# Layer 0's conditioning in its paired products: two places, half steps, an earlier start

## The chip, the cores and the metric

The kernel runs on one core of one Trainium2 chip. The metric is the device time of one execution in microseconds (us). The engines are TensorE (PE; its weight loads are shown as PEld), VectorE (DVE), ScalarE (ACT), GpSimd (POOL) and SyncE (SP). Transfers are issued from a queue of SP, ACT or POOL, and each engine and each queue works in its own fixed order.

## The reference

One inference step of a two-layer trunk over 640 tokens (512 latent tokens and 128 prompt tokens) of width 2048. In each layer, in outline:

```
sh, sc, gt = split(silu(cond) @ ada_w[layer] + ada_b[layer], 3)   # cond: one row for the prompt, one for the latents
h = rms_norm(x, norm_g[layer]) * (1 + sc) + sh
y = mixer(h @ w_in)          # layer 0: windowed attention, and a gated width-3 convolution
x = x + gt * (y @ w_out)     # layer 1: differential attention, and grouped attention
```

The part that matters here is the first line, the *conditioning*: two rows of 2048 numbers times a matrix of 2048 x 6144 per layer, which has to be read whole from HBM (50 MB a layer). Its result for layer 1 is needed only when layer 1's `h` is made.

## The kernel before, in words

**Projections.** The large products multiply 128 x 128 weight tiles by 320 token columns at a time (two halves of the 640 tokens). For accuracy each factor is split into a high and a low part: ACT rounds the weights to `wh` (L292), DVE subtracts to get `wl` (L293), and PE forms three products per tile. Layer 0's input projection first runs as *single tiles* (`run_tiles`): one column block of 128 at a time, four *quarters* of 24 matmuls each. The last nine twice-wide column blocks run as *pairs* (`run_pairs`): two column blocks at once, with seven products M1, M5, M6, M2, M7, M3, M4 in the place of eight, in that order. Each product has 24 matmuls over 320 columns (L612 to L614) in two halves. Some products need sums of weights, which DVE makes: L551 for M5, L554 and L556 for M6 and M7, L563 for M3. A pair loads its weights into tiles of the tag `w8` (four places) and of `raw`.

**The order of the work.** The kernel is written as Python generators. After each quarter of a single tile, and after each half of a pair's product, `slot()` is called. It advances `prep` (what follows a tile), then `attn` (attention, or here `forms`, which prepares moving operands for the pairs), and then a *filler* `fill`: `credit` grows by `rate`, and for each whole unit of credit one step of the filler is written out. The order on each engine follows from the order in which instructions are written and from when a scheduler thinks that they can run; it is fixed when the kernel is built. Low parts of weights are written three quarters, or three half products, ahead of their use (`SPLIT_AHEAD`), raw weights of single tiles five quarters ahead.

**The turn.** At single tile `n_turn` of layer 0 (L471) six single tiles are left: four gates, one `u` and one `c`. There `tail_turn` (L1338) empties the first filler, closes one pool of tiles and opens the next, `mid`, with five places of the tag `xr`, and queues `forms`. The filler's rate becomes 0 for these six tiles. The gates take three `xr` tiles each. In the last of the six, `twist` (L1347) overwrites half of `h` with `t1`, for which part of the constant tile `tables` is used.

**The conditioning beside the pairs.** `ada_slow` (L265) is the filler of the pairs, with a rate of 0.33. It computes two blocks of 512 columns for layer 1. For each of 16 weight tiles of 128 x 512 (256 KB) of a block, one step does two DVE operations, one for each of the two conditioning rows: L279 for the first weight tile, L281 for the others:

```
V.scalar_tensor_tensor(out=acc[c], in0=w, scalar=sT[:, kt, c:c + 1], in1=acc[c],
                       op0=ALU.mult, op1=ALU.add)
```

and then fetches the next weight tile through POOL's queue (L270) into the same place `w`, a part of `tables`. After a block `ada_fold` (L224) sums the accumulators over the partitions on PE (L229), copies the sums on ACT, turns them on PE (L235) and adds the bias on DVE. At M6 of the last pair `tail_tail` (L1392) writes out whatever is left of the filler, and queues the first four tiles of the output projection's operand (`late_yin`, L1181), which take `xr` places too.

Of the kernel before, what the change touches and what calls it, by code (L numbers as in the profile page):

```python
# [15 lines left out]
ALU = mybir.AluOpType  # L16
# [6 lines left out]
KT = D // P  # L23
# [3 lines left out]
HALF = NT // 2  # L27
# [23 lines left out]
FILL0_FROM = 6  # L51
# [5 lines left out]
def trunk_kernel(ctx: ExitStack, tc: tile.TileContext, I: dict, O: dict):  # L57
# [206 lines left out]

    def ada_slow(blocks):  # L265

        w = tables[:, 3 * HALF:3 * HALF + 512]

        def fetch(l, cb, kt):
            nc.gpsimd.dma_start(w, I["ada_w"][l, kt * P:(kt + 1) * P, cb * 512:(cb + 1) * 512])  # L270

        fetch(*blocks[0], 0)
        yield
        for b, (l, cb) in enumerate(blocks):
            acc = [xr_tile(f"acc{c}")[:, 0:512] for c in range(2)]
            for kt in range(KT):
                for c in range(2):
                    if kt == 0:
                        V.tensor_scalar(acc[c], w, sT[:, kt, c:c + 1], None, ALU.mult)  # L279
                    else:  # L280
                        V.scalar_tensor_tensor(out=acc[c], in0=w, scalar=sT[:, kt, c:c + 1], in1=acc[c],  # L281
                                               op0=ALU.mult, op1=ALU.add)
                if kt + 1 < KT:
                    fetch(l, cb, kt + 1)
                elif b + 1 < len(blocks):
                    fetch(*blocks[b + 1], 0)
                yield
            ada_fold(l, cb, acc, pools["cur"], "xr", 5)
            yield

    def split(hi, lo, x):
        A.activation(hi, x, AF.Copy)  # L292
        V.tensor_sub(lo, x, hi)  # L293
# [73 lines left out]
    def slot(fill=None, rate=0.0, steps=1.0):  # L367
        settle_late()
        advance(prep, len(prep))
        pace[0] += steps  # L370
        while pace[0] >= 1.0:
            advance(attn, 1)
            pace[0] -= 1.0
        credit[0] += rate
        while credit[0] >= 1.0:
            next(fill, None)
            credit[0] -= 1.0

    def run_tiles(jobs, w_ap, make_h, fill=None, rate=0.0, ahead=None, order=(0, 1, 2, 3), before=None,
# [89 lines left out]
        for i in range(lead, len(jobs)):  # L469
            fn = jobs[i][1]  # L470
            if turn and i == turn[0]:  # L471
                drain(prep)
                turn[1]()
                rate = 0.0
            pp = new_pp((i - lead) % 2)
            if twist and i == len(jobs) - 1:
                for hv in (HV[1:], HV[:1]):
                    for qd in range(4):
                        proj_q(pp, parts[t + qd], qd, qd, hv)
                        run_ahead(t + 1)  # L480
                        slot(fill, rate / 2, steps(i) / 2)
                    if hv[0][0]:
                        twist()
                drain(prep)
                begin(fn, pp)
                return (i - lead) % 2
            split_last = last is not None and i == len(jobs) - 1
            for qd in range(4):
                proj_q(pp, parts[t], qd, qd, HV[:1] if split_last else HV)
                if before and qd == 0:  # L490
                    before(i)
                t += 1
                run_ahead(t)
                if pending and not prep:
                    n = pending.pop(0)
                    begin(jobs[n][1], pps[n])
                slot(fill, rate if t > fill_from else 0.0, steps(i))
            if split_last:
                first = last(pp, 0)
                next(first)  # L500
                for qd in range(4):
                    proj_q(pp, parts[t - 4 + qd], qd, qd, HV[1:])
                    next(first, None)
                for _ in last(pp, 1):
                    pass
                return
            drain(prep)
            if i >= lead + grace and pending:
                settle()
            if lp and not pending and not prep:  # L510
                lp.__exit__(None, None, None)
                lp = None
            begin(fn, pp)
# [2 lines left out]

    GROUP = {"M1": "M1", "M6": "M1", "M7": "M1", "M4": "M1", "M5": "M5", "M3": "M5", "M2": "M2"}

    def run_pairs(cols, w_ap, mov, room, used, begin, done, tail, fill=None, rate=0.0):


        ap = pools["cur"]
# [79 lines left out]
        for i, (p, name) in enumerate(seq):  # L602
            if name in ("M1", "M5", "M2"):
                bank = {"M1": f"pa{(used + p + 1) % 2}", "M5": f"pb{1 - used}", "M2": f"pb{used}"}[name]
                banks[name] = pproj.tile([P, 512], F32, tag=bank, name="pq")[:, 0:HALF]
            ps, rows_ = banks[GROUP[name]], mov[MOV[name]]
            first, final = name in GROUP.values(), name in ("M4", "M3", "M2")
            for h in range(2):
                wh, wl = parts[2 * i + h]
                for j in range(4):  # L610
                    hi, lo = rows_(4 * h + j)
                    PE.matmul(ps, wh[:, j, :], hi, start=(first and h == 0 and j == 0), stop=False, skip_group_check=True)  # L612
                    PE.matmul(ps, wh[:, j, :], lo, start=False, stop=False, skip_group_check=True)  # L613
                    PE.matmul(ps, wl[:, j, :], hi, start=False, stop=(final and h == 1 and j == 3),  # L614
                              skip_group_check=True)
                if h == 0:
                    ahead(2 * i + 1)
                    slot(fill, rate)
            after(p, name, ps)
            ahead(2 * i + 2)  # L620
            if name == "M1":
                load(p + 1, "A11")
            elif name == "M6":
                load(p + 1, "A21")
                load(p + 1, "A22")
            elif name == "M7":
                load(p + 1, "A12")
            if p == len(cols) - 1:
                tail(name)
            slot(fill, rate)  # L630

    def stage(ap, pp):
        s = ap.tile([P, NT], F32, tag="stg", name="stg", bufs=2)
# [499 lines left out]
    def forms(src):  # L1133

        f = None

        def load(j):
            if src is None:
                for k, n in ((j, "acc"), (j + 8, "sq")):
                    V.tensor_add(st[n], *hs[k])  # L1140
                return st["acc"], st["sq"]
            ts = [big("w8", bufs=4)[:, 0:NT] for _ in range(2)]
            for i in range(2):
                nc.sync.dma_start(ts[i], src[j + 8 * i])
            return ts

        T.clear()
        t1.clear()
        nxt = load(0) if src else None
        for j in range(8):  # L1150
            (ya, yb), nxt = nxt or load(j), (load(j + 1) if src and j < 7 else None)
            b11, b12, b21, b22 = ya[:, 0:HALF], ya[:, HALF:NT], yb[:, 0:HALF], yb[:, HALF:NT]
            x = big("sx")[:, 0:3 * HALF]
            if f is None:
                f = big("sf")
            d = room[j] if j < 4 else f[:, (j - 4) * HALF:(j - 3) * HALF] if j < 7 else b11
            x2, x3, x4 = (x[:, i * HALF:(i + 1) * HALF] for i in range(3))
            V.tensor_sub(x3, b22, b12)
            V.tensor_add(x2, b11, x3)
            V.tensor_sub(x4, b21, x2)  # L1160
            V.tensor_sub(d, b12, b11)
            t = big(f"T{j}", dtype=F32R).rearrange("p (s n) -> p s n", s=2)
            split(t[:, 0, :], t[:, 1, :], x)
            T.append(t)
            t1.append(d)
            yield
# [119 lines left out]
    def xr_tile(name):  # L1286
        return pools["cur"].tile([P, NT], F32, tag="xr", name=name, bufs=5)
# [50 lines left out]
    def tail_turn():  # L1338
        drain(attn)
        for _ in fill0:  # L1340
            pass
        close("even")
        open_pool("mid")
        st["acc"], st["sq"] = (pools["cur"].tile([P, NT], F32, tag=n, name=n) for n in ("acc", "sq"))
        attn.append(forms(None))

    def twist():  # L1347
        drain(attn)
        for j in range(8):
            hi, lo = hs[j]  # L1350
            split(hi[:, HALF:NT], lo[:, HALF:NT], t1[j])

    used = run_tiles(jobs, I["ev_w_in"][0], h0_maker, fill0, FILL0, ada_group, trans=TRANS, grace=GRACE,
                     cut=((0, 2), (2, 4)), summed=keep, led=even_start, lead_in=lambda: ada_on_pe(0, 0, 0, 2),
                     steps=lambda i: 0.4 if i >= n_turn else 1.35 if i > last_q else 1.0,
                     turn=(n_turn, tail_turn), twist=twist, fill_from=FILL0_FROM)

    tails = [("b", "h", 3)] + [x for i in range(4, 8) for x in (("u", "c", i), ("b", "h", i))]
    srcs = {}
# [32 lines left out]
    def tail_tail(name):  # L1392
# [7 lines left out]
        elif name == "M3":  # L1400
            for n in range(2):
# [2 lines left out]
    run_pairs([(EV[a] + i * P, EV[b] + i * P) for a, b, i in tails], I["ev_w_in"][0],  # L1404
              {"B11": half_of(0, 0), "T1": half_of(0, 1), "B21": half_of(8, 0), "B22": half_of(8, 1),
               "T2": form_of(0), "T3": form_of(1), "T4": form_of(2)}, room, used, tail_begin, tail_done, tail_tail,
              fill0b, 0.33)
    drain(prep)

    def y0_maker(k):  # L1410
# [410 lines left out]
```

## Time and profile before

| what | us |
|---|---|
| median of 3 runs | 2278.35 (2276.54 to 2283.84) |
| profiled execution | 2275.12 |
| its span, first to last instruction | 2273.3 |
| PE busy in it | 2230.9 (98%) |
| DVE busy in it | 1712.6 (75%) |
| layer 0's last six single tiles, about | 567 to 653 |
| layer 0's pairs | 653.4 to 887.1 |

Times inside the profile are counted from the span's start. In a row of a view, "L281 DVE" is the source line and the engine, `out<-in` are the kernel's names of tiles, and what stands in square brackets is the time that the engine stood idle just before, and what ended it. Instructions are pipelined, so that the next one can start a little before the end that is shown for the one before. The mean granted clock of PE in this execution was 0.996.

### The profile page before, as it was taken

The page shows a single profiled execution, that of the slowest core. Times are in us where ns is not written, and L with a number is a line of the kernel's source. Part 1 is how long each engine was busy: PE and PEld are TensorE (multiplying, and loading weights), DVE is VectorE, ACT ScalarE, POOL GpSimd, SP SyncE. Part 2 cuts the span into 40 slices and gives each one's busy share as a digit, 9 for nine tenths or more (in the row PEclk, how much of TensorE's full clock was granted, in tenths as well). Part 3 has the DMA queues.
Part 4 walks back from the last instruction along what each step waited for, and adds up shares of the span by engine and source line. Part 5 has one row for each costly group of instructions (what it writes and reads, how often), then busy time and mean ns, then how long its engine had stood idle before and what let it go on. Part 6 is the DMA issues. An engine that isn't in the chain of part 4 may idle for free.

```text
span 2273.3 us, 41407 instructions
## 1 busy us (share of the span) xinstructions
PE 2230.9 (98%) x15708; PEld 2156.4 (95%) x15708; DVE 1712.6 (75%) x3197; ACT 1109.6 (49%) x2293; POOL 225.3 (10%) x337
## 2 busy tenths in 40 slices
PE   7999999999999999999999999999999999999999
PEld 5889999999999999999999999999999999999999
DVE  4659899988868898887776764858658778676665
ACT  4335554544333435444644445566665554554443
POOL 2220000000001000000200000010010111111010
PEclk9999999999999999999999999999999999999999
DMA  9985556564534447743763334423324234237541
GB/s 357 340 284 156 175 171 204 164 188 151 157 100 130 135 122 227 210 140 113 246 211 115 108 110 141 132 71 99 94 76 145 76 115 131 78 114 245 168 134 49
DMA packets 385607, 351.43 MB, mean 155 GB/s; under 512 B 18162, under 2 KB 342224, under 8 KB 384896
## 3 DMA queue, kind: packets, MB, share of 16 engines
q1 hardware_dynamic: 369008, 289.76, 42.5%
q0 software_dynamic: 15536, 56.80, 7.2%
q8 instruction: 123, 2.02, 0.4%
q10 hardware_dynamic: 864, 2.23, 0.3%
q14 instruction: 76, 0.62, 0.1%
HBM read 305.86 MB, written 42.86 MB: 153 GB/s over the span
## 4 chain that ended last, share of the span: by engine, by line
PE 50%; DVE 6%; ACT 3%; issue 2%; DMA 2%; POOL 1%; ACTq 0%; DVEq 0%; POOLq 0%; SPq 0%
PE pq L612 8%; PE pq L613 8%; PE pq L614 8%; PE pb L328 3%; PE pb L327 3%; PE pa L329 3%; PE pb L329 3%; PE pa L328 3%; PE pa L327 3%; DVE acc L218 1%; PE T L642 1%; PE T L815 1%; DMA adaw<-in_ada_w 1%; DVE nm L789 1%; ACT p L796 1%
## 5 line engine op out<-in xcount | busy, mean ns | idle before, releaser
L292 ACT ACTIVATE wh<-raw 128x512 fp32r<-128x512 f32 (+1 forms) x400 | 241.1, 604 | 393.5 <-PE pb L328 277.3
L327 PE MATMUL pa<-h,wh 128*128 128x320 f32 x1216 | 388.7, 320 | 0.4 <-DVE sum L416 0.4
L328 PE MATMUL pa<-h,wh 128*128 128x320 f32 x1216 | 379.0, 312 | 1.5 <-DVE h L293 1.5
L327 PE MATMUL pb<-h,wh 128*128 128x320 f32 x1216 | 378.1, 311 | 0.9 <-ACT h L292 0.9
L329 PE MATMUL pa<-h,wl 128*128 128x320 f32 x1216 | 377.9, 311 | 0.0
L329 PE MATMUL pb<-h,wl 128*128 128x320 f32 x1216 | 377.8, 311 | 0.0
L328 PE MATMUL pb<-h,wh 128*128 128x320 f32 x1216 | 377.4, 310 | 0.0
L293 DVE TENSOR_TENSOR wl<-raw,wh 128x512 fp32r<-128x512 f32 (+1 forms) x400 | 261.2, 654 | 142.2 <-ACT wh L292 126.5
L612 PE MATMUL pq<-h,wh 128*128 128x320 f32 x896 | 277.4, 310 | 0.0
L614 PE MATMUL pq<-h,wl 128*128 128x320 f32 x896 | 277.1, 309 | 0.0
L613 PE MATMUL pq<-h,wh 128*128 128x320 f32 x896 | 276.6, 309 | 0.0
L327 PEld LDWEIGHTS pa<-h,wh 128*128 128x128 f32 x1216 | 228.9, 188 | 10.6 <-issue 9.7
L328 PEld LDWEIGHTS pa<-h,wh 128*128 128x128 f32 x1216 | 229.3, 189 | 6.5 <-issue 4.5
L327 PEld LDWEIGHTS pb<-h,wh 128*128 128x128 f32 x1216 | 229.5, 189 | 2.1 <-ACT h L292 1.1
L329 PEld LDWEIGHTS pa<-h,wl 128*128 128x128 f32 x1216 | 228.8, 188 | 1.6 <-issue 1.6
L328 PEld LDWEIGHTS pb<-h,wh 128*128 128x128 f32 x1216 | 229.4, 189 | 0.4 <-issue 0.4
L329 PEld LDWEIGHTS pb<-h,wl 128*128 128x128 f32 x1216 | 229.2, 188 | 0.4 <-issue 0.4
L612 PE MATMUL pq<-T,wh 128*128 128x320 f32 x672 | 209.3, 311 | 3.4 <-ACT wh L292 1.8
L614 PE MATMUL pq<-T,wl 128*128 128x320 f32 x672 | 208.3, 310 | 2.7 <-DVE wl L293 2.7
L613 PE MATMUL pq<-T,wh 128*128 128x320 f32 x672 | 208.2, 310 | 0.0
L258 DVE SCALAR_TENSOR_TENSOR acc<-adaw,sT,acc 128x1024 f32<-128x1024 f32 x150 | 189.1, 1275 | 0.0
L292 ACT ACTIVATE wh<-sx 128x512 fp32r<-128x512 f32 x168 | 105.1, 632 | 151.7 <-PE pq L613 96.2
(375 smaller groups left out, 4682.7 us busy)
## 6 DMA issues: line engine op xcount, KB each, us to landing
adaw<-in_ada_w SPq DMA_DIRECT2D x80, 512.0 KB, 4.0
raw<-in_od_w_in SPq DMA_DIRECT2D x160, 256.0 KB, 3.0
raw<-in_ev_w_in SPq DMA_DIRECT2D x130, 256.0 KB, 3.5
ada<-in_ada_w SPq DMA_DIRECT2D x11, 2048.0 KB, 13.5
adaw<-in_ada_w SPq DMA_DIRECT2D x128, 128.0 KB, 2.4
w<-in_ev_w_in SPq DMA_DIRECT2D x27, 512.0 KB, 3.9
w<-in_od_w_in SPq DMA_DIRECT2D x24, 512.0 KB, 4.0
adah<-in_ada_w SPq DMA_DIRECT2D x20, 512.0 KB, 9.2
```

The source lines that it names most:

```text
L218: V.scalar_tensor_tensor(out=a, in0=w, scalar=sT[:, kt, c:c + 1], in1=a, op0=ALU.mult, op1=ALU.add)
L258: V.scalar_tensor_tensor(out=acc[c], in0=w, scalar=sT[:, kt, c:c + 1], in1=acc[c], op0=ALU.mult, op1=ALU.add)
L292: A.activation(hi, x, AF.Copy)
L293: V.tensor_sub(lo, x, hi)
L327: PE.matmul(ps, wh[:, i, :], hi[:, sl], start=(j == js[0] if alone else (pos == 0 and j == 0)), stop=False)
L328: PE.matmul(ps, wh[:, i, :], lo[:, sl], start=False, stop=False)
L329: PE.matmul(ps, wl[:, i, :], hi[:, sl], start=False, stop=(j == js[1] - 1 if alone else (pos == 3 and j == 3)))
L612: PE.matmul(ps, wh[:, j, :], hi, start=(first and h == 0 and j == 0), stop=False, skip_group_check=True)
L613: PE.matmul(ps, wh[:, j, :], lo, start=False, stop=False, skip_group_check=True)
L614: PE.matmul(ps, wl[:, j, :], hi, start=False, stop=(final and h == 1 and j == 3), skip_group_check=True)
L642: PE.transpose(t[:, i * P:(i + 1) * P], src(b), ident)
L789: V.tensor_reduce(nm, s, axis=AX.X, op=ALU.max, negate=True)
```

## The change

`ada_slow` gets two places instead of one and fetches two weight tiles ahead. Its places depend on the time: until `twist` it takes a new `w8` tile for each fetch (`st["adaw"]`), and after that it alternates between the old place in `tables` and one `xr` tile. One step is now one DVE operation instead of two (a *half step*), and a new fetch is written after the second of a weight tile.

`run_tiles` no longer sets the rate to 0 at the turn: it takes a new filler and rate from `turn`, here `fill0b` (this `ada_slow`) and 0.7, so that the conditioning begins beside the last six single tiles. `run_pairs` no longer takes a rate: it advances the filler by one half step in each of the two slots of the products named in `rests`, here M6, M2 and M3, and not in the others.

```
     def ada_slow(blocks):
-        w = tables[:, 3 * HALF:3 * HALF + 512]
-        def fetch(l, cb, kt):
+        todo = [(l, cb, kt) for l, cb in blocks for kt in range(KT)]
+        places, ws = [], []
+        def fetch():
+            if not todo:
+                return
+            l, cb, kt = todo.pop(0)
+            if "adaw" in st:
+                w = st["adaw"]()
+            else:
+                if not places:
+                    places.extend([tables[:, 3 * HALF:3 * HALF + 512], xr_tile("adaw")[:, 0:512]])
+                w = places[0]
+                places.reverse()
             nc.gpsimd.dma_start(w, I["ada_w"][l, kt * P:(kt + 1) * P, cb * 512:(cb + 1) * 512])
-        fetch(*blocks[0], 0)
+            ws.append(w)
+        fetch()
+        fetch()
         yield
-        for b, (l, cb) in enumerate(blocks):
+        for l, cb in blocks:
             acc = [xr_tile(f"acc{c}")[:, 0:512] for c in range(2)]
             for kt in range(KT):
                 for c in range(2):
                     if kt == 0:
-                        V.tensor_scalar(acc[c], w, sT[:, kt, c:c + 1], None, ALU.mult)
+                        V.tensor_scalar(acc[c], ws[0], sT[:, kt, c:c + 1], None, ALU.mult)
                     else:
-                        V.scalar_tensor_tensor(out=acc[c], in0=w, scalar=sT[:, kt, c:c + 1], in1=acc[c],
+                        V.scalar_tensor_tensor(out=acc[c], in0=ws[0], scalar=sT[:, kt, c:c + 1], in1=acc[c],
                                                op0=ALU.mult, op1=ALU.add)
-                if kt + 1 < KT:
-                    fetch(l, cb, kt + 1)
-                elif b + 1 < len(blocks):
-                    fetch(*blocks[b + 1], 0)
-                yield
+                    if c:
+                        ws.pop(0)
+                        fetch()
+                    yield
             ada_fold(l, cb, acc, pools["cur"], "xr", 5)
             yield
...
 (run_tiles)
             if turn and i == turn[0]:
                 drain(prep)
-                turn[1]()
-                rate = 0.0
+                fill, rate = turn[1:3]
+                turn[3]()
...
 (run_pairs)
-    def run_pairs(cols, w_ap, mov, room, used, begin, done, tail, fill=None, rate=0.0):
+    def run_pairs(cols, w_ap, mov, room, used, begin, done, tail, fill=None, rests=()):
...
-                    slot(fill, rate)
+                    slot(fill, float(name in rests))
...
 (tail_turn)
+        st["adaw"] = lambda: big("w8", bufs=4)[:, 0:512]
         attn.append(forms(None))
...
 (twist)
+        st.pop("adaw")
...
-                     turn=(n_turn, tail_turn), twist=twist, fill_from=FILL0_FROM)
+                     turn=(n_turn, fill0b, 0.7, tail_turn), twist=twist, fill_from=FILL0_FROM)
...
-              fill0b, 0.33)
+              fill0b, ("M6", "M2", "M3"))
```

More of the change, by code (lines that the diff above doesn't have):

```diff
@@ L629, in run_pairs @@
                 tail(name)
-            slot(fill, rate)
+            slot(fill, float(name in rests))
     def stage(ap, pp):
```

## The prediction

> **What bounds the kernel now.** I read the page first, then busy time by stretch, then the waits of the engine that fell behind, then its timeline at a loss.
>
> ```profile
> span 2273.3 us, 41407 instructions
> PE 2230.9 (98%) x15708; PEld 2156.4 (95%) x15708; DVE 1712.6 (75%) x3197; ACT 1109.6 (49%) x2293; POOL 225.3 (10%) x337
> ```
>
> TensorE (PE) is the bound, so the change is worth only the PE time that it gives back. I cut the touched part at the starts of its nine pairs. The first row is the single tiles from shortly after their turn; the others are pairs 0 to 8 of layer 0. The columns are the width, then busy us and instruction count per engine, then the granted clock.
>
> ```profile
> core 0: us, PE busy (x) PEld busy (x) DVE busy (x) ACT busy (x) POOL busy (x), PEclk, DMA share, GB/s
> 571.00:653.40 82.40, 82.40 (x564) 82.40 (x563) 61.95 (x104) 29.03 (x49) 3.24 (x6) 1.00 0.47 139
> 653.40:678.00 24.60, 24.60 (x170) 24.60 (x169) 22.21 (x37) 10.87 (x19) 2.16 (x4) 1.00 0.41 115
> 678.00:706.20 28.20, 26.73 (x170) 26.20 (x169) 23.17 (x37) 9.89 (x18) 3.23 (x6) 0.94 0.50 146
> 706.20:730.80 24.60, 24.60 (x170) 24.60 (x169) 22.52 (x37) 10.78 (x19) 1.84 (x4) 1.00 0.40 118
> 730.80:759.10 28.30, 26.16 (x180) 25.00 (x179) 22.35 (x36) 10.26 (x19) 2.46 (x5) 1.00 0.43 125
> 759.10:783.80 24.70, 24.70 (x171) 24.70 (x170) 22.65 (x38) 10.89 (x19) 2.15 (x4) 1.00 0.38 111
> 783.80:809.20 25.40, 24.81 (x169) 24.58 (x169) 21.66 (x34) 10.01 (x18) 3.23 (x6) 1.00 0.49 147
> 809.20:836.90 27.70, 25.76 (x171) 24.70 (x170) 24.46 (x40) 10.57 (x19) 2.15 (x4) 1.00 0.39 115
> 836.90:862.50 25.60, 25.60 (x180) 25.00 (x179) 21.31 (x35) 10.28 (x19) 1.62 (x3) 1.00 0.51 156
> 862.50:887.10 24.60, 24.60 (x170) 24.60 (x170) 22.94 (x39) 17.15 (x29) 0.00 (x0) 1.00 0.57 174
> ```
>
> An undisturbed pair takes 24.60 us (pairs 0, 2 and 8). The others exceed it by 3.6, 3.7, 0.1, 0.8, 3.1 and 1.0, together 12.3 us. Two of them (3 and 7, with some ten instructions more) contain a fold of the conditioning, which is work and stays:
>
> ```profile
> 754.73 0.64 PE L229 MATMUL T<-acc,ones 128*32 128x256 f32 x8
> 756.58 0.38 PE L235 MATMUL T<-ident,ada_sb 128*128 128x128 f32 x2
> ```
>
> A fold is 0.64 + 0.38 = 1.02 us, two are 2.0, so **10.3 us of PE time are lost in the pairs**. The cause is on VectorE (DVE): the one place for a conditioning weight.
>
> ```profile
> DVE acc L281 <- DMA tables<-in_ada_w: 18.7, 19, 2.2
> L281 DVE SCALAR_TENSOR_TENSOR acc<-tables,sT,acc 128x512 f32<-128x512 f32 x60 | 43.8, 747 | 18.8 <-DMA tables<-in_ada_w 18.7
> L279 DVE TENSOR_SCALAR acc<-tables,sT 128x512 f32<-128x512 f32 x4 | 1.9, 480 | 0.0
> ```
>
> DVE stood still 19 times, 18.7 us in all, at the head of its queue for a weight to land. All of this falls in pairs 0 to 7. Their DVE busy times average 22.54 us; with 18.7 / 8 = 2.3 us of waiting that is 24.9 us against 24.6 us of PE work. DVE has nothing left, and what it queues behind the wait comes late:
>
> ```profile
> 680.52 1.42 DVE L281 SCALAR_TENSOR_TENSOR acc<-tables,sT,acc 128x512 f32<-128x512 f32 x2 [1.71 <-DMA tables<-in_ada_w]
> 681.85 0.48 DVE L1380 SCALAR_TENSOR_TENSOR acc<-sq,pq 128x320 f32<-128x320 f32 x1
> 682.25 0.68 DVE L293 TENSOR_TENSOR wl<-sx,wh 128x512 fp32r<-128x512 f32 x1
> 682.85 0.82 DVE L1382 TENSOR_TENSOR CV<-CV,acc 128x640 f32<-128x640 f32 x1
> 683.59 1.22 DVE L554 TENSOR_TENSOR sx<-sx,w 128x1024 f32<-128x1024 f32 x1
> 685.20 1.41 DVE L281 SCALAR_TENSOR_TENSOR acc<-tables,sT,acc 128x512 f32<-128x512 f32 x2 [0.40 <-DMA tables<-in_ada_w]
> 686.53 1.29 DVE L293 TENSOR_TENSOR wl<-sx,wh 128x512 fp32r<-128x512 f32 x2
> ...
> 685.58 0.41 PE L612 MATMUL pq<-T,wh 128*128 128x320 f32 x1 [0.34 <-ACT wh L292]
> 687.27 0.42 PE L614 MATMUL pq<-T,wl 128*128 128x320 f32 x1 [1.13 <-DVE wl L293]
> ```
>
> Ahead of M6's weight sum (L554) and its low part stand two waits (1.71 + 0.40) and four conditioning operations (1.42 + 1.41). PE then waits for exactly that high and low part: pair 1's loss.
>
> **The change part by part.** *Two places.* A fetch takes this long:
>
> ```profile
> L270 POOL DMA_DIRECT2D tables<-in_ada_w x32: 536/536/545, 642.7 to 843.9; - x32
> DMA to landing us min/median/max: 2.8/3.1/4.1
> ```
>
> Today it is issued after a step's second operation, for the next step three half-product slots on; a slot is 24.6 / 14 = 1.76 us, so 5.3 us are left and DVE's running order eats the margin. With two places a fetch goes out two weights ahead. In the pairs, the shortest way from fetch to use is from the end of M6 to the middle of M3, over M2 and M7: five slots, 8.8 us against at most 4.1. The 18.7 us of DVE waiting go.
>
> *Fewer and spread steps.* The generator now yields 67 times: one start, 64 half steps, two folds. By the code the turn leaves 0.2 of credit (82 slots at 2.1), and 20 slots at 0.7 and 8 at 0.35 add 16.8: 17 calls beside the single tiles, hence 16 half steps. The pairs call it in M6, M2 and M3 only, six times a pair: 48 half steps less one in pairs 0 to 7, then the last half step, a fold, and the drain after pair 8's M6. In pairs 0 to 7 the DVE load other than conditioning is 22.54 - (43.8 + 1.9) / 8 = 16.8 us; six operations at 0.747 make it 21.3 us of 24.6, with no wait inside. M4's end, M1 and M5, where all three large losses began, hold none. In M3, M2 and M7 a backlog of a few tenths is possible; the low parts are made three half products ahead (5.3 us), which covers it. If that cover were gone, each 0.1 us would cost 0.1 on PE. Of the 10.3 us I let 1.5 stay lost (pair 5, which has the smallest DVE load and still lost 0.8 us, is the nearest row).
>
> *The moved half steps.* Beside the single tiles PE is full (82.40 of 82.40), so whatever DVE delays there is a new loss.
>
> ```profile
> 571.00:617.00 46.00, 46.00 (x316) 46.00 (x315) 43.60 (x74) 17.00 (x26) 2.16 (x4) 1.00 0.60 178
> 617.00:653.40 36.40, 36.40 (x250) 36.40 (x249) 18.35 (x32) 12.03 (x23) 1.08 (x2) 1.00 0.30 89
> ```
>
> The half steps cost 2 x 0.48 + 14 x 0.747 = 11.4 us; DVE has 82.4 - 61.95 = 20.4 us free, but only 2.4 until 617, where forms() fills it. At 0.7 in a slot of 3.5 us, 46 us take some 9 half steps, 6.7 us: forms() ends about 4 us later than now (at 617), still ahead of the twist near 641. Low parts have three quarters, 10.5 us, of lead. I put this at 0, with 0 to 4 us as bounds. The 10 fetches (0.54 us each) go through POOL's queue past the gates' stores, an engine with 3.24 us busy in 82; 0.
>
> *w8 places.* The early fetches use the four places of the pairs' own weights, which four loads take long ahead today:
>
> ```profile
> 574.87 1.05 SPq L527 DMA_DIRECT2D w<-in_ev_w_in  x2
> 578.22 2.54 SPq L527 DMA_DIRECT2D w<-in_ev_w_in  x2
> ...
> w<-in_ev_w_in SPq DMA_DIRECT2D x23, 512.0 KB, 3.9
> ...
> L292 ACT ACTIVATE wh<-raw 128x512 fp32r<-128x512 f32 (+1 forms) x400 | 241.1, 604 | 393.5 <-PE pb L328 277.3
> ```
>
> Two are now held by conditioning until about 652, so A12 of pair 0 loads then and lands at about 656 to 658; its halves are split from about 660 for M2 at 664. Covered by some 3 us; 0, and if the 17th call slips behind the first M6 slot (662) it costs up to 662 + 3.9 + 1.3 - 664 = 3.2 us (load, then high part 0.60 and low part 0.65). SP's queue behind that load holds raw weights five quarters ahead.
>
> *The end.* The second fold moves from 851 to after pair 8's M6 (about 14 us before the pairs end), and its accumulators free the places of the first y tiles later. Now those are done early:
>
> ```profile
> 868.09 1.55 DVE L293 TENSOR_TENSOR h<-yin,h 128x640 fp32r<-128x640 f32 x2
> 873.24 0.81 DVE L293 TENSOR_TENSOR h<-yin,h 128x640 fp32r<-128x640 f32 x1
> ```
>
> 13 us before the projection needs them at 887. Fold, load and splits move them some 10 us; 3 us stay. Cost 0, up to 3. Each fold now follows its last half step by one slot, not three: PE may wait for DVE, between 0 and 1.76 us each; I take 0.4 each, as DVE has slack then.
>
> *Sum*: -10.3 + 1.5 + 0.8 = **-8.0 us**. The profiled execution took 2275.1 us (span 2273.3); the median shown is 2278.35, 3.2 above, and the saving is the same: 2278.35 - 8.0 = **2270.3 us**.
>
> One part of the 10.3 is clock. Pair 1's PE idled 28.20 - 26.73 = 1.5 us but lost 3.6: its granted clock was 0.94, so about 0.06 x 28.2 = 1.7 us went to slower matmuls; pair 3 idled longer (2.1 us) at 1.00. I take the drop as the wait's doing. The Trainium skill, TensorE: Matmul & The Clock Gate, "What's actually happening", says that the clock halves only after an idle window of about 3.4 us that runs freely; by that 1.5 us would not be enough, and the sum would be -6.3. This hangs on it: rival C.
>
> **The rivals.** *A, the steps are not moved* (25%). If pair loads take all w8 places first, nothing is fetched beside the single tiles, and DVE keeps 22.5 us per pair without waits: 92%. Or DVE still lags and M6 and M3 keep waiting. For: the four loads above go out at the turn. Against: the first fetches stand earlier in the program. About half the loss returns: -4, **2274**, with 2271.5 to 2279 around it.
>
> *B, ready half steps crowd M6* (17%, the slower side). With weights landed two ahead, nothing but DVE's written order holds half steps back. Four of them ahead of L554 cost 3.6, 2.7 (3.7 less a fold) and 3.1 us in pairs 1, 3 and 6. If the order puts four there in all eight pairs, the price is 8 x 3.1 = 25 us at most, or 8 x (3.1 - 2.1) = 8 us when only the waits of pair 1 (2.1 us) fall away: between 2 us faster and 15 slower, middle +6.5, **2285**. It decides at 10.3 / 8 = 1.3 us lost per pair. For and against:
>
> ```profile
> L1140 DVE TENSOR_TENSOR acc<-h x8: 815/818/819, 573.8 to 614.4; 128x640 f32<-128x640 f32 x8
> 760.47 0.48 DVE L279 TENSOR_SCALAR acc<-tables,sT 128x512 f32<-128x512 f32 x1
> 745.89 0.54 POOL L270 DMA_DIRECT2D tables<-in_ada_w  x1 [4.96 <-DVE acc L281]
> ```
>
> forms() at 0.4 in a slot should take 8.8 us a form; it took (614.4 - 573.8) / 7 = 5.8, so it ran ahead of its slots. The second block's first half step, whose weight was fetched at 745.9, waited until 760.5, near its slot.
>
> *C, the clock drop has another cause* (5%): 1.7 us stay, **2272**.
>
> **How the numbers follow.** 0.3% (6.8 us) is about what a measurement of this kernel can tell from no change. Forecast 53%, own range 2267 to 2271.5 (nearly the whole 10.3 recovered, down to 6.8); A and C 30%, within 0.3%; B 17%, slower. The likeliest is 2270.3. The range goes from 2265.5 (all 10.3 and a run-to-run 2.5) to 2282, which leaves out B's upper half and little else.
>
> **What would show it.** Right: no waits of the conditioning operation for its weight in the pairs, every pair near 24.6 us plus folds, DVE busy about 21 us in each, 16 of 64 half steps before 653, PE still full there. Wrong: PE idle in the single tiles; M2 of pair 0 waiting for A12; low parts late at M6 with half steps ahead of them; a gap near the end of pair 8.

## The result, and the profile after

| | before | after |
|---|---|---|
| median, 20 runs each | 2279.06 us (2274.37 to 2283.84) | 2274.50 us (2269.31 to 2280.82) |
| ratio | | 0.9978, 95% interval 0.9970 to 0.9986 |
| second comparison, 14 and 5 runs | 2278.58 us | 2270.00 us, ratio 0.9964 (0.9951 to 0.9978) |
| third comparison, 23 and 12 runs | 2278.73 us | 2275.72 us, ratio 0.9989 (0.9978 to 1.0000) |
| profiled execution (the first) | 2275.12 us | 2276.43 us |

The changed kernel is faster by 5.0 us (3.2 to 6.8) in the first comparison, with 8.0 forecast. In the second it gains 8.2, in the third 2.5, with an interval that reaches no change. The first profiled execution of before lies below its kernel's median and that of after above its own, so their spans are not compared; their stages are.

Busy time by stretch of the changed kernel, cut as in the prediction: two stretches of single tiles, then pairs 0 to 8 (width; busy us and count for PE, PEld, DVE, ACT, POOL; granted clock; DMA share; GB/s):

```profile
571.00:617.00 46.00, 46.00 (x316) 46.00 (x315) 43.75 (x74) 16.14 (x25) 6.47 (x12) 1.00 0.56 177
617.00:653.60 36.60, 36.60 (x251) 36.60 (x250) 29.94 (x51) 12.93 (x24) 2.69 (x5) 1.00 0.57 169
653.60:678.20 24.60, 24.60 (x170) 24.60 (x169) 24.30 (x40) 11.11 (x19) 2.15 (x4) 1.00 0.44 130
678.20:702.90 24.70, 24.70 (x171) 24.70 (x170) 18.82 (x28) 10.02 (x19) 1.62 (x3) 1.00 0.40 120
702.90:728.50 25.60, 25.60 (x180) 24.99 (x179) 21.64 (x37) 11.47 (x20) 1.07 (x2) 1.00 0.32 93
728.50:753.10 24.60, 24.60 (x170) 24.60 (x169) 22.94 (x36) 10.09 (x18) 3.76 (x7) 1.00 0.58 174
753.10:779.30 26.20, 25.13 (x170) 24.61 (x169) 26.05 (x43) 10.88 (x19) 2.69 (x5) 1.00 0.45 131
779.30:803.90 24.60, 24.60 (x170) 24.60 (x169) 19.97 (x30) 10.01 (x18) 1.08 (x2) 1.00 0.37 110
803.90:828.50 24.60, 24.60 (x170) 24.60 (x169) 19.12 (x30) 11.11 (x19) 0.00 (x0) 1.00 0.30 87
828.50:853.20 24.70, 24.70 (x171) 24.70 (x170) 17.22 (x25) 10.06 (x18) 0.54 (x1) 1.00 0.27 83
853.20:878.80 25.60, 25.60 (x180) 24.99 (x180) 20.35 (x35) 16.44 (x28) 0.00 (x0) 1.00 0.53 164
```

The pairs now take 225.2 us where they took 233.7: -8.5. Pairs 2 and 8 hold the folds (1.0 each); only pair 4 still loses time, 1.6 us. PE stays full beside the single tiles. DVE's waits for a weight in this part (engine and line, waited for: us, times, longest) have gone from 18.7 us to

```profile
DVE acc L294 <- DMA adaw<-in_ada_w: 1.8, 1, 1.8
DVE acc L294 <- DMA tables<-in_ada_w: 1.0, 2, 0.5
```

But DVE's load is uneven, 24.3 and 26.05 us in pairs 0 and 4 and 17.2 in pair 7, where an even spread was forecast. The groups of half steps by place, with the first and last start, show why:

```profile
L294 DVE SCALAR_TENSOR_TENSOR acc<-tables,sT,acc x24: 742/745/752, 645.9 to 788.2; 128x512 f32<-128x512 f32 x24
L294 DVE SCALAR_TENSOR_TENSOR acc<-adaw,sT,acc x20: 743/746/753, 659.2 to 784.6; 128x512 f32<-128x512 f32 x20
L294 DVE SCALAR_TENSOR_TENSOR acc<-w,sT,acc x16: 741/744/748, 590.0 to 636.9; 128x512 f32<-128x512 f32 x16
```

The last half step starts at 788.2, in pair 5; its slot is in pair 8. With weights landed ahead, half steps stand in DVE's order far ahead of their slots: 20 of 64 ran before 653 (16 forecast) and the rest in bunches. One bunch is pair 4's loss, in DVE's timeline:

```profile
753.25 0.75 DVE L294 SCALAR_TENSOR_TENSOR acc<-adaw,sT,acc 128x512 f32<-128x512 f32 x1 [1.81 <-DMA adaw<-in_ada_w]
...
756.18 0.74 DVE L294 SCALAR_TENSOR_TENSOR acc<-tables,sT,acc 128x512 f32<-128x512 f32 x1
756.85 1.93 DVE L1343 SCALAR_TENSOR_TENSOR CV<-U,vec,CV 128x511 f32<-128x511 f32 x4
758.69 1.22 DVE L566 TENSOR_TENSOR sx<-sx,w 128x1024 f32<-128x1024 f32 x1
759.83 0.74 DVE L294 SCALAR_TENSOR_TENSOR acc<-tables,sT,acc 128x512 f32<-128x512 f32 x1
760.49 0.75 DVE L294 SCALAR_TENSOR_TENSOR acc<-adaw,sT,acc 128x512 f32<-128x512 f32 x1
761.15 1.29 DVE L305 TENSOR_TENSOR wl<-sx,wh 128x512 fp32r<-128x512 f32 x2
...
761.89 0.42 PE L626 MATMUL pq<-T,wl 128*128 128x320 f32 x1 [0.65 <-DVE wl L305]
```

It is before's picture of pair 1 again: a wait, then half steps on both sides of M6's sum (now L566), and PE waits for M6's low part (and 0.42 us for its high part just before).

### The profile page after: what moved, and what is told of

It reads as the page before. It is cut to its first block, busy times and chain, and to the rows that moved or that the text cites. A ratio compares the mean times of both kernels' runs of the same rounds, so it can differ in the third digit from the quotient of the medians.

```text
span 2274.7 us, 41401 instructions
## 1 busy us (share of the span) xinstructions
PE 2231.4 (98%) x15708; PEld 2158.1 (95%) x15708; DVE 1714.8 (75%) x3197; ACT 1111.0 (49%) x2293; POOL 223.9 (10%) x337
## 4 chain that ended last, share of the span: by engine, by line
PE 81%; DVE 7%; DMA 4%; ACT 4%; issue 3%; POOL 1%; SPq 0%; DVEq 0%; ACTq 0%; POOLq 0%
PE pq L625 10%; PE pq L626 10%; PE pq L624 10%; PE pa L339 6%; PE pa L340 6%; PE pb L340 6%; PE pb L339 6%; PE pb L341 6%; PE pa L341 6%; PE T L827 2%; DMA adaw<-in_ada_w 1%; DVE acc L218 1%; PE S L839 1%; PE T L178 1%; PE T L654 1%
## 5 line engine op out<-in xcount | busy, mean ns | idle before, releaser
L339 PEld LDWEIGHTS pa<-h,wh 128*128 128x128 f32 x1216 | 229.1, 188 | 10.3 <-issue 9.3
```

Of the source, the lines that this page charges most:

```text
L339: PE.matmul(ps, wh[:, i, :], hi[:, sl], start=(j == js[0] if alone else (pos == 0 and j == 0)), stop=False)
```

## The experiments

All kernels' pairs and totals are in one table behind the single accounts. Two theories were open after the result. D/W: the pairs' loss was DVE's queue, above all its waits for the one place. S or O: what the total lacks against the pairs (8.5 saved there, 5.0 in all) is either the run (S) or a slower order later on (O).

**The conditioning left out** of the changed kernel:

```
-    fill0b = ada_slow([(1, 2), (1, 3)])
+    fill0b = iter(())        # and these two parts of mod[1] set to zero
```

> The changed kernel without the conditioning of the two blocks: neither weights nor multiplications nor folds, the values set to zero. Theory D (DVE's queue was what PE waited for in the pairs): pairs at 9 x 24.6 = 221.5 us, no wait of PE in them, and a total 4 us below the changed kernel (two folds of 1.02, pair 4's 1.6). Rival P (PE's losses in the pairs come from the pairs' own sums and splits): some pairs stay 1 to 3 us above 24.6.

Total 2267.5 us, ratio 0.9952 (0.9939 to 0.9964). The stretch of all nine pairs:

```profile
655.10:876.70 221.60, 221.60 (x1515) 221.60 (x1514) 168.38 (x259) 101.62 (x177) 2.17 (x4) 1.00 0.35 105
```

221.6 us, PE full, the clock at 1.00. D holds: without the conditioning, the pairs' own sums and low parts cost PE nothing. The total is 2.5 us below the changed kernel's in the same comparison (2270.00), where 4 were expected.

**Two places alone** in the kernel before: whole steps at 0.33 a slot, beside the pairs only. The edit is the change's `fetch`, with the two later places only.

> The kernel before with two places for the weights and nothing else: whole steps at 0.33 a slot, only beside the pairs. Theory D with the waits as the main part: DVE's waits for weights in the pairs fall from 18.7 us to below 3, DVE is busy 22.5 us a pair, pairs lose 2 to 5 us in place of 10.3, total 5 to 8 us below before in the pairs. Rival B (ready half steps crowd ahead of M6's sum): waits gone but 8 us or more still lost in the pairs, as whole steps of two operations now stand there whenever DVE looks free.

Pairs 225.0 us, total 2270.56 us, ratio 0.9967 (0.9954 to 0.9979). DVE's waits for weights, and pair 2, the only one that lost time beside the folds:

```profile
DVE acc L291 <- DMA adaw<-in_ada_w: 1.6, 2, 0.8
703.80:729.80 26.00, 25.10 (x169) 24.58 (x169) 25.12 (x41) 10.89 (x19) 2.69 (x5) 1.00 0.47 142
```

This is the changed kernel's saving from one of its three parts. Against *tied* below, in which PE never waits (223.6), 1.4 us are still lost. A second profile gave 226.3, so 2.7 lost, which is within the 2 to 5 that were expected.

**Half steps alone**, with one place and beside the pairs only:

```
-                yield                        # after both operations and the fetch
+                    yield                    # after each operation
-            slot(fill, rate)
+            slot(fill, 1.35 * (name in rests))   # rests = M6, M2, M3
```

> The kernel before with half steps in M6, M2 and M3 and nothing else: one place, pairs only, 1.35 half steps a slot there. Theory W (the second place does it all, since it takes away the waits): DVE still waits 12 to 19 us for weights in the pairs, the pairs take 230 to 234 us, total within 3 us of before. Rival H (the finer, better placed steps help by themselves): pairs below 227.

Pairs 234.7 us, total 2283.08 us, ratio 1.0018 (1.0008 to 1.0028): slightly slower than before. DVE's waits grew from 18.7 us; pairs, total and waits all lie above what was expected:

```profile
DVE acc L281 <- DMA tables<-in_ada_w: 23.8, 25, 2.8
```

**The earlier start alone**, with one place at a time and whole steps:

```
+                fill, rate = turn[1:3]       # rate 0.35 beside the single tiles, a fresh w8 tile for each fetch
-              fill0b, 0.33)
+              fill0b, 0.24)
```

> The kernel before with the earlier start and nothing else: one place at a time, whole steps, 0.35 a slot beside the single tiles and 0.24 in the pairs. Theory W: the waits are about as many per step, with a quarter of the steps gone from the pairs, so 10 to 15 us of DVE waiting, pairs 228 to 232 us, single tiles without a new PE wait. Rival E (the pairs are short of DVE time, and any step moved out frees them): pairs below 227.

Pairs 233.7 us, total 2277.73 us, ratio 0.9993 (0.9984 to 1.0003). The expected 228 to 232 us was missed: 18 waits, as many as before within one, but longer. PE stays full beside the single tiles.

```profile
DVE acc L282 <- DMA tables<-in_ada_w: 29.6, 18, 3.6
660.00:893.70 233.70, 227.23 (x1534) 222.40 (x1534) 192.45 (x309) 99.93 (x179) 13.99 (x26) 1.00 0.42 125
```

DVE is busy 192 us in the pairs in place of 203, and PE loses as much. But the waits grew by 10.9 us (18.7 to 29.6) as the work fell by 10.8 (203.3 to 192.5), so this run does not tell what less work with equal waits would give. It shows that an earlier start with one place frees nothing. That the waits are the cost rests on the two places: there DVE is as busy as before (203.0 us in the pairs), its waits are 1.6 us, and 8.7 of the pairs' 233.7 us are gone.

**Half steps in M4, M1 and M5** in place of M6, M2 and M3:

```
-              fill0b, ("M6", "M2", "M3"))
+              fill0b, ("M4", "M1", "M5"))
```

> The changed kernel with the half steps in M4, M1 and M5 in place of M6, M2 and M3. In DVE's written order the half steps stand ahead of their slots, and almost at the same places as in the changed kernel. Theory F (ready half steps are written when DVE looks free, the slots hardly count): pairs 224.5 to 227.5 us, total equal to the changed kernel within 2 us. Rival R (the choice of products matters): M5 and M6 lose 1 us or more in most pairs, pairs above 229.

Pairs 225.3 us, total 2269.25 us, ratio 0.9966 (0.9953 to 0.9979): as the changed kernel, and pair 4 lost 1.7 us again. DVE's order as built is nearly the same. Each line below begins with a pair's M6 sum (6); 3 is M3's sum, f the sum for M7, 5 one half of M5's, w a low part, * a half step:

```
changed, pairs 0 to 5          M4, M1, M5 instead             tied (next experiment)
6ww*w3w**w*wfw*w55w*w*w*w*w**w   6ww*w3w**w*wfw*w55w*w*w*w*w**w   6ww3ww*w*wf*ww*w55w*ww*ww
6*www3wwwfww55wwwwww             6*www3wwwfww55wwwwww             6ww3ww*w*wf*ww*5w5w*w*www
6ww3wwwwfww55www***w*w**w        6ww3wwwwfww55wwwww****w          6ww3ww*w*wf*ww*w55ww*www
6**www3w**w*w*fww*5w5w**w*w*w*w* 6**www3w*w**w*fww*5w5w**w*w*w*w* 6ww3ww*w*wf*ww*5w5w*w*www
6**wwww3w**w*wfw5w5w*w*w*w**w    6**wwww3w*w*fw*w*w5w5w*w*w**w    6ww3ww*w*wf*ww*w55w*ww*ww
6ww*3w*w*wwfww55wwwwww           6**www3w*w**wfww55wwwwww         6ww3ww*w*wf*ww*5w5w*w*www
```

The choice of products changed the pairs by 0.1 us. By this order, a half step whose weight and accumulator are ready seems to be written wherever DVE looks free to the scheduler.

**Half steps tied to their slots** by a value that is made there:

```
+                    sc = sT[:, kt, 2 + c:3 + c]
+                    V.scalar_tensor_tensor(out=sc, in0=mark[0], scalar=0.0, in1=sT[:, kt, c:c + 1],
+                                           op0=ALU.mult, op1=ALU.add)      # mark[0]: a column of the newest low part
```

and `sc` as the half step's scalar.

> The changed kernel with each half step tied to its slot: its scalar is first copied by a DVE operation of one column that also reads the newest low part (64 operations of about 0.15 us more). In DVE's written order the half steps then stand in M6, M2 and M3 of all nine pairs, none between M6's sum and M6's low parts. Theory F, with rival B of the prediction as what is left: pair 4's 1.6 us go, all pairs 24.6 plus two folds, 223.6 us, 1 to 2 us less than the changed kernel. Rival: the even load of DVE loses about 0.2 us in each pair, pairs 225 us or more.

The nine pairs, in one stretch:

```profile
654.80:878.40 223.60, 223.60 (x1534) 222.38 (x1534) 201.39 (x353) 101.27 (x177) 13.45 (x25) 1.00 0.42 126
```

223.6 us: PE does not wait once, although DVE does 64 operations more than in the changed kernel. DVE's wait for a weight is gone too, so pair 4's 1.6 us were the bunch together with its wait; which of the two cost more is not separated. Total 2272.05 us, ratio 0.9969 (0.9959 to 0.9979), so the total does not follow.

**Second and third profiles** of both kernels, and *tied* and *places* again beside the changed kernel:

> The kernel before, a second profile. Theory S (the pairs' loss is in the written order, so it repeats; what differs after the pairs is partly the run): pairs again 233 to 235 us against 233.7, and the time from the end of the pairs to the end of the span, 1386.2 us in the first profile, comes out anywhere from 1385 to 1393. Theory O (the part after the pairs became slower by its new written order): that part repeats within 1 us, 1385 to 1387.

> The changed kernel, a second profile and five rounds. Both theories: pairs 225 to 226 us against 233.7 before. Theory S: the part after the pairs, 1395.9 us in its first profile, falls to 1388 to 1393, and the total is about 0.9975 of before. Theory O: it stays at 1395 to 1397.

> The kernel before, a third profile. Theory S (what differs after the pairs is the run): pairs 232 to 235 us, and from the pairs' end to the span's end 1382 to 1392 us, as the changed kernel's runs also give. Theory O (the changed kernel's part after the pairs is slower by 2 us or more because its order in layer 1 is written otherwise): 1382 to 1387 here, above that in the next run.

> The changed kernel once more. Pairs 225 to 226 us. Theory S: total 0.9965 to 0.9975 of before, the pairs' 7 to 8.5 us nearly whole. Theory O: 0.9975 to 0.9985.

> The tied half steps once more, on one chip with the changed kernel. Pairs 223.6 us. If the pairs' time is all that counts: 1.5 to 2.2 us below the changed kernel. If the 64 small operations or what follows the pairs take it back: the same within 1 us.

> The kernel before with two places alone, once more, on one chip with the changed kernel. If the second place is the whole gain: pairs 225 to 226 us and a total within 1.5 us of the changed kernel. If the half steps and the earlier start add to it: 2 us or more above the changed kernel.

The time from the pairs' end to the span's end is 1386.2, 1385.9 and 1390.2 us in the three profiles of before and 1395.9, 1388.0 and 1391.8 in those of the changed kernel. The signs set above do not decide between S and O by it: before's third and the changed kernel's second profile lie where S puts them, and the changed kernel's third ratio, 0.9989, lies above the ranges of both.

All runs, with the pairs' time in each profile, and the ratio times 2278.6 us less 2278.6 as the total's difference. The last three columns are for layer 1's single tiles, which run after layer 0's output projection and layer 1's own first pairs. "Order" tells which of two orders DVE's last 42% of instructions have (1343 in the kernel before). Order 2 is the same in every kernel marked 2. By the times of before's first profile the two differ only from 1550 to 1990 us, where 377 of the 1343 positions hold another instruction. From the same start on, PE's orders too differ in that part alone. "To matmul 2764" is the time from the start of the stage to its 2764th of 3456 projection matmuls (80%). "Where orders differ" is the time from the last PE instruction ahead of that part to the first behind it.

| kernel | pairs, us | pairs against 234.1 | total against before, us | order | to matmul 2764, us | where orders differ, us |
|---|---|---|---|---|---|---|
| before | 233.7, 232.6, 236.0 | | | 1 | 619.9, 618.8, 619.5 | 439.6, 437.8, 439.0 |
| two places alone | 225.0, 226.3 | -8.4 | -7.5, -8.4 | 1 | 620.3, 618.3 | 439.8, 437.9 |
| earlier start alone | 233.7 | -0.4 | -1.6 | 1 | 621.2 | 440.4 |
| changed | 225.2, 225.8, 225.2 | -8.7 | -5.0, -8.2, -2.5 | 2 | 624.9, 621.8, 621.7 | 442.1, 441.7, 441.4 |
| M4, M1, M5 | 225.3 | -8.8 | -7.7 | 2 | 622.6 | 441.9 |
| tied | 223.6, 223.6 | -10.5 | -7.1, -7.5 | 2 | 622.6, 621.2 | 441.9, 440.7 |
| half steps alone | 234.7 | +0.6 | +4.1 | 2 | 621.4 | 440.6 |
| none | 221.6 | -12.5 | -10.9 | 2 | 620.7 | 440.8 |

The pairs' times repeat within 0.6 us in the changed kernel. In the kernels of order 1 the total follows the pairs within 1.2 us. In those of order 2 it falls short, by 1.1 to 3.5 us in four of them and by 3.7, 0.5 and 6.2 in the changed kernel's three comparisons; layer 1's stage takes 622.1 us there on average and 619.7 in order 1. No line that makes layer 1's instructions was edited. Presumably another filler beside the pairs changes, two stages on, which of two ready instructions is written first; how is not shown. Two waits of PE in that stage, in the changed kernel's first profile:

```profile
1603.16 0.44 PE L839 MATMUL S<-k1h,q0h 128*128 128x384 f32 x1 [0.96 <-ACT p L808]
1721.59 0.38 PE L891 MATMUL T<-ptl,vh 128*128 128x256 f32 x1 [0.40 <-DVE ptl L305]
```

Over the part where the orders differ, PE's waits for that line of ACT (the softmax's exponentials) and for DVE's `on` are, first in the changed kernel and then in the kernel before, which has none for `on`:

```profile
PE S L839 <- ACT p L808: 2.9, 4, 1.0
PE T L1601 <- DVE on L1596: 1.2, 1, 1.2
PE S L827 <- ACT p L796: 0.7, 3, 0.4
```

All profiles agree in this: 1.8 to 2.9 us for the exponentials in order 2 and 0.7 to 1.3 in order 1, and the wait of 1.2 us for `on` in order 2 alone.

So theory O holds, at 2.3 us: where the orders differ, the six profiles of order 1 take 437.8 to 440.4 us and the eight of order 2 take 440.6 to 442.1. These ranges lie close, and no kernel exchanged that order alone. Theory S holds beside it. In the stretch from the pairs' end to that part, and in the one behind it, where no such difference of order is seen but at the start of the output projection, the means of the two groups agree within 0.6 us, but single profiles spread by 5.5 and 4.5 us. The changed kernel has the same order each time, so that its three shortfalls range from 0.5 to 6.2 us comes from the run or the chip (the second and third comparison ran on different chips).

*Places*, expected within 1.5 us of the changed kernel, was 6.4 us faster in the third comparison (2269.32 and 2275.72; its ratio to before 0.9963, 0.9950 to 0.9975) and 0.6 us slower in the second (2270.56 and 2270.00). So these runs do not settle which of the two is faster; they show that the half steps and the earlier start add no gain to the second place that can be seen. *Tied* came out 4.1 us below the changed kernel in the third comparison, more than either expectation had, and not below the two places.

## Why the prediction was right or wrong

*The time: in the range, but where a rival stood.* 2274.5 us is outside the forecast's own 2267 to 2271.5, and all but equal to rival A's 2274, though A did not happen. The saving of 0.22% is below the 0.3% that I had given more than half of the chances to exceed. What shows the forecast's mechanism is the pairs' time, not the total.

*The loss and its cause: right.* 10.3 us were lost in the pairs to DVE's wait for one place; 8.7 went, averaged over three profiles of each kernel (8.8 forecast, with 1.5 left over). The waits fell from 18.7 to 2.8 us.

*The half steps: wrong in the mechanism, right in the sum.* The term "fewer and spread steps" held six half steps a pair at M6, M2 and M3. In the profile they run up to three pairs early, none is left for pairs 6 to 8, and in pair 4 rival B happened, at 1.6 us once and not in eight pairs. The 1.5 us that I kept as lost are met by that, not by the backlog in M7 and M3 that I had named: that is luck. The row I took as nearest for it was misread: pair 5 has not the smallest DVE load, since pair 7 has 21.31 us and lost nothing beside its fold. B's condition (ready half steps ahead of their slots) came true in every pair that had any; its price was wrong. Half steps around M6's sum cost PE where a wait for a weight stood ahead of them (pair 4 here, pair 2 of the two places with 0.74 us of it); pair 3 here and pairs 4 and 6 of the two places hold two half steps right behind the sum without a wait, and lost nothing. The "against" row I quoted, the second block's first half step near its slot, was read wrongly: in the kernel before, one place kept everything near its slot.

*The moved half steps: right.* PE stayed full beside the single tiles (82.6 of 82.6 us). But this part, too, gained nothing: alone it left the pairs at 233.7.

*w8 places: the premise was wrong, the cost of 0 right.* I had two places held; the fetches took all four at the turn, and the pairs' own loads went out from 626 on. The rows of POOL's queue and of SP's:

```profile
572.64 2.24 POOL L281 DMA_DIRECT2D w<-in_ada_w  x4
626.36 0.37 SPq L539 DMA_DIRECT2D w<-in_ev_w_in  x1
```

Pair 0 still ran in 24.6 us. Rival A, in which the pairs' loads take the places first, was the reverse of what happened.

*The end: undersized.* I took 0.8 us for folds and the last pair. The folds did not wait (0.64 and 0.38 us as before), but in some profiles of the changed and the tied kernel PE waits once in the output projection for a low part, 0.4 to 1.0 us, and the projection's first 600 matmuls take 0.6 to 1.8 us longer than the 88.1 us of the kernel before:

```profile
928.25 0.42 PE L341 MATMUL pb<-h,wl 128*128 128x320 f32 x1 [1.01 <-DVE wl L305]
```

*The term that was missing*, in the sum's -8.0 against -5.0, is the written order of a stage that the change does not touch: 2.3 us. The rest is within the spread from run to run. I had costed everything after the pairs' end at 0 to 3 us at that end, and nothing in layer 1.

*The clock, rival C: it falls.* All of the changed kernel's pairs have a clock of 1.00 in the profile above. In the kernel before, its drop comes and goes with the run, in pairs that wait; pair 3 of the third profile, with the waits it always has:

```profile
733.90:764.10 30.20, 27.97 (x181) 26.57 (x180) 22.91 (x37) 10.26 (x19) 2.69 (x5) 0.94 0.41 118
```

In the first profile the same pair took 28.3 us at 1.00. So a drop costs about 1.9 us, and the 1.7 us of rival C did not stay. This speaks against the rule of the Trainium skill (TensorE: Matmul & The Clock Gate, "What's actually happening") that I had weighed, that an idle window of about 3.4 us comes before a drop: PE stood idle 2.2 us here in all. Which waits bring a drop is open: *early*, where DVE waits longest, has none in the pairs of its profile.

## What to carry to other kernels

An operation that waits for a transfer at the head of an engine's queue costs by what is queued behind it, so in these runs the second place was worth what half steps and an earlier start were not; look for the wait before thinning out the work. A place in the program is only a wish where a scheduler writes the order: what must stand in a slot needs a value that is made there. And when a few us are at stake, compare the order of the stages that were not edited, since it can change and take part of the gain.

## What the runs showed of the hardware

PE's clock dropped (0.94 over a stretch of 28 to 30 us) after waits that sum to 1.5 to 2.2 us, in some executions and not in others of the same kernel. In the first profile of before, PE had waited 0.34 us at 685.6 and 1.13 us at 687.3; from 688.5 to 691.7 twelve matmuls then start 0.27 us apart, and 0.15 apart before and after. And in layer 1's output projection, behind its single tiles, PE waited for "issue", that is for nothing that the profile shows, in ten of the fourteen profiles of all kernels, by 1.4 to 3.1 us:

```profile
2126.01 1.30 PE L654 MATMUL T<-ident,xr 128*128 128x128 f32 x5 [3.06 <-issue]
```

It comes in both orders, and is a part of the spread of some 10 us between runs of one kernel.
